# A hybrid decoder block: the output gate as four rounded-format matmuls, the three per-head sums as two each, and v centred while it is transposed

## The chip, the core and the metric

The kernel runs on one NeuronCore of one Trainium2 chip. The metric is the device time of one execution in microseconds (us); the time of before is the median of three runs.

## The reference, cut to what matters

One decoder block: an adaLN-modulated RMS norm, one input projection, two mixers side by side (RWKV-7 on 1024 channels, multi-window pooling on 1024), an output projection, a second norm, a gated MLP with a depthwise convolution, and a final norm. There are 512 tokens, a model width of 2048 and an MLP width of 5632, all in fp32. The change touches the RWKV-7 mixer (16 heads of 64 channels):

```python
kk = heads(k * k_k)
kk = kk / max(sqrt(sum(kk * kk, per head)), 1e-12)          # sum 1
...
y = _wkv7_scan(r, decay, k, v, -kk, kk * a)                 # per head a 64x64 state, linear in v
mean = mean(y, per head); var = mean((y - mean)**2, per head)   # sum 2
y = (y - mean) * rsqrt(var + 64e-5) * ln_w + ln_b
bonus = sum(r * k * r_k, per head) * v                      # sum 3
out = (y + bonus) * (sigmoid(xg) @ g2)                      # the gate; xg has 160 columns
```

## The kernel before

Channels lie on the 128 partitions, tokens along the free dimension, so a tile is 128x512. Two number formats go into TensorE. Plain fp32 operands are used as they are. Large projections use the rounded format fp32r: a weight tile is split into a rounded value `whi` (ScalarE cast, L106) and a remainder `wlo` (VectorE subtraction, L108), activations likewise, and one product is three matmuls of 512 columns (`mm3`, L111 to L114).

The program has three stages. First (L168 to L258) the modulation vectors are made on VectorE, x is normalised, and the first eight tiles of the input projection are summed in the eight PSUM banks `pf`. At its end (L235 to L258) ScalarE and VectorE empty those banks: the token-shifted `xwa`, `xg1`, `xg2` (the gate's 128 + 32 columns, through a sigmoid), the r, k, v tiles of the first pair, and two pooling inputs `upad`. The PSUM pool of the next stage takes over the same banks.

The second stage, from there to about 800 us, works through eight pairs of heads (p = 0 to 7). Per pair:
- `stage_a` (L358): loads the pair's LoRA weights `lw` (two buffers), makes the decay, then k's norm: square `sq` (ScalarE, L389), its sum over each head as a matmul with a block matrix of ones (`bones`, L391), Ln and Exp (L394, L395), then `ar`, `bt`, `nt`. A DRAM round trip and a serial chain of small VectorE operations (L421 to L430) invert a triangular part. The bonus is a second sum with `bones` (L449) times v.
- `stage_b` (L455): small matmuls that finish the inverse.
- `stage_c` (L511): four chunks of 128 tokens. Each transposes v, `bt`, `kt` (L520), multiplies by masks (L531) and carries the state. The result gathers in the PSUM tile `py` (tag "y"). Then the tail: copy `py` to SBUF (L577), subtract the head mean as a matmul with `cent` (L579), square (L581), sum with `bmean` (L583), Ln and Exp (L585, L586), scale (L587, L588), add the bonus (L589); the gate is two fp32 matmuls into the PSUM tile of tag "ch" (L591, L592), which the sum of L583 used just before; multiply (L593) and store to DRAM (L594).

Beside the pairs run the 27 remaining tiles of the input projection (`win_tile`, L314: 48 matmuls `mm` each) and the rest of the modulation vectors on VectorE (`ada_rest`, L334). The pairs' code stands under a high priority (L618); a scheduler fixes each engine's order before the run, and puts the `mm` matmuls where it finds room. Every engine works through its list strictly in that order, and so does SP, from which all DMAs are issued. Scratch tiles of the pairs come from one pool tag, `ring`, with seven buffers (L232).

The third stage, to the end at 2450 us, is the output projection, the MLP and the last norm; all of it is `mm3` work.

Of the kernel before, what the change touches and what calls it, by code (L numbers as in the profile page):

```python
# [9 lines left out]
F32 = mybir.dt.float32  # L10
F32R = mybir.dt.float32r
# [5 lines left out]
P = 128  # L17
T = 512
# [36 lines left out]
def block_kernel(ctx, tc, a, out, stop=None, dbg=None):  # L55
# [8 lines left out]
    nc.sync.dma_start(vec, a["vec"][:, :])  # L64
    cmat = cp.tile([P, 5, P], F32, tag="cmat", name="cmat")
    nc.sync.dma_start(cmat, a["cmat"][:, :, :])
    ident, bones, bmean, cent, ones = (cmat[:, i, :] for i in range(5))
    masks = cp.tile([P, 4, P], F32, tag="masks", name="masks")
    nc.sync.dma_start(masks, a["mask4"][:, :, :])
    mlev = cp.tile([P, 2, 64], F32, tag="mlev", name="mlev")  # L70
# [98 lines left out]
    if True:  # L169
# [53 lines left out]
        if True:  # L223
            def shift(ps, m, dst):
                S.activation(dst, ps, AF.Copy, scale=drv[:, m : m + 1])
                V.scalar_tensor_tensor(dst[:, 1:T], ps[:, 0 : T - 1], col("mu", m), dst[:, 1:T],
                                       op0=ALU.mult, op1=ALU.add)

            def ring(name):
                return ring16(name)[:, 16:]  # L230

            def ring16(name):  # L232
                return ra.tile([P, 16 + T], F32, tag="ring", name=name, bufs=7)
# [4 lines left out]
            xg1 = ra.tile([P, T], F32, tag="xg1", name="xg1")  # L238
            shift(pf[1], 25, xg1)
            S.activation(xg1, xg1, AF.Sigmoid)  # L240
            xg2 = ra.tile([P, T], F32, tag="xg2", name="xg2")
            shift(pf[2], 26, xg2)
            S.activation(xg2, xg2, AF.Sigmoid)

# [113 lines left out]
    def stage_a(p, rkv):  # L358
# [28 lines left out]

        sq = ring("sq")
        S.activation(sq, k, AF.Square, scale=col("kk", p))  # L389
        psn = atile()  # L390
        PE.matmul(psn, bones, sq, start=True, stop=True)  # L391
        inv = ring("inv")
        V.tensor_scalar_max(inv, psn, 1e-24)
# [17 lines left out]
        for h in range(2):  # L411
            V.tensor_mul(ntv[:, h, :, :], ch(pss[h]), masks[:, 0:1, :].to_broadcast([P, NC, P]))
        dn = tc.dram_tile([32, 32, 32], F32, name=f"dn{p}")
# [34 lines left out]
        psb = atile()  # L448
        PE.matmul(psb, bones, k2, start=True, stop=True)  # L449
        bv = q.bv = ra.tile([P, T], F32, tag="bv", name="bv", bufs=2)  # L450
# [60 lines left out]
    def stage_c(p, q):  # L511
        ar, bt, kt, v, y2 = q.ar, q.bt, q.kt, q.v, q.y2
        py = ctile("y")
        st = None
        for c in range(NC):
            cl = slice(c * P, (c + 1) * P)

            pst = btile()
            for i, src in enumerate((v, bt, kt)):
                PE.transpose(pst[:, i * P : (i + 1) * P], src[:, cl], ident)  # L520
# [9 lines left out]
            for h in range(2):  # L530
                V.tensor_mul(lc[:, h, :, :], pss[h][:, 0:384].rearrange("p (i t) -> p i t", i=3), masks[:, 1:4, :])  # L531

# [42 lines left out]

        y = ra.tile([P, T], F32, tag="post", name="y", bufs=2)
        S.copy(y, py)  # L577
        pyc = ctile("y")
        PE.matmul(pyc, cent, y, start=True, stop=True)  # L579
        sq = ra.tile([P, T], F32, tag="post", name="sqy", bufs=2)  # L580
        S.activation(sq, pyc, AF.Square)  # L581
        pv = ctile("ch")
        PE.matmul(pv, bmean, sq, start=True, stop=True)  # L583
        rs = ra.tile([P, T], F32, tag="post", name="rs", bufs=2)
        S.activation(rs, pv, AF.Ln, bias=eps[:, 1:2])  # L585
        S.activation(rs, rs, AF.Exp, scale=-0.5)  # L586
        V.tensor_mul(rs, pyc, rs)  # L587
# [3 lines left out]
        PE.matmul(pg, q.lw[:, 1, :], xg1, start=True, stop=False)  # L591
        PE.matmul(pg, q.lw[0:32, 2, :], xg2[0:32, :], start=False, stop=True)  # L592
        V.tensor_mul(rs, rs, pg)  # L593
# [294 lines left out]
def pack(x, c, w_ada, b_ada, norm1_g, w_in, mu_shift, w0, w2, a0, a2, g2, k_k, k_a, r_k, ln_x_w, ln_x_b,  # L888
# [16 lines left out]
    mu = np.zeros(27 * P, f)  # L905
    mu[: 3360] = A(mu_shift[0])
    put("mu", mu)
    put("w0", w0[0]); put("a0", a0[0]); put("kk", k_k[0]); put("ka", k_a[0]); put("rk", A(r_k[0]).reshape(-1))
# [17 lines left out]
    for i, n in enumerate(WIN_ORDER):  # L926
        w = 32 if n == "T2" else P
        blk[i, :, :, :w] = wi[:, starts[n] : starts[n] + w].reshape(KT, P, w)
    o["win0"] = C(blk[:8].transpose(1, 2, 0, 3)).reshape(KT, P, 8 * P)
# [15 lines left out]
    lora[:, :, 1, :] = A(g2[0])[:128].reshape(P, NP, P).transpose(1, 0, 2)  # L945
    lora[:, 0:32, 2, :] = A(g2[0])[128:].reshape(32, NP, P).transpose(1, 0, 2)
    o["lora"] = lora
# [4 lines left out]
    bo = (i[:, None] // 64 == i[None] // 64).astype(f)  # L952
    o["cmat"] = C(np.stack([eye, bo, bo / f(64), eye - bo / f(64), np.ones((P, P), f)], 1))
    lt = (i[:, None] < i[None]).astype(f)
    le = (i[:, None] <= i[None]).astype(f)
    o["mask4"] = C(np.stack([lt, le, lt, le], 1))
    ml = np.zeros((P, 2, 64), f)
# [26 lines left out]
```

## Time and profile before

| | us |
|---|---|
| median of 3 runs (2449.73 to 2455.32) | 2451.7 |
| profiled execution, its own time | 2452.14 |
| its span, first to last instruction | 2450.0 |
| TensorE (PE) busy in the span | 2347.1 |
| PE weight loads (PEld), which overlap | 1872.0 |
| VectorE (DVE) busy | 1408.7 |
| ScalarE (ACT) busy | 874.6 |

So 2.1 us of the profiled execution lie outside its span. A matmul's recorded length runs on into the next one, since matmuls are pipelined: the price of one is read from the distance between starts, not from its length. An fp32 matmul leaves two records, an fp32r matmul one, a transpose one. A number in square brackets behind a row of the timeline is the idle time ahead of it and who ended it.

### The profile page before, as it was taken

Reading aid. Unit: us, or ns where it says so; the run is one execution under the profiler, and the core shown is the slowest. Engines: PE = TensorE matmul, PEld = TensorE weight load, DVE = VectorE, ACT = ScalarE, POOL = GpSimd, SP = SyncE. Lnnn points to the kernel's source line nnn. Section 1 sums busy time; section 2 is a strip of 40 time slices with the busy share of each in tenths; the row PEclk is TensorE's granted clock in tenths of the full one; section 3 lists DMA queues with packets and bytes.
Section 4 is the critical chain, followed back from the end, with each engine's and each line's share of the span. In section 5 each row is a group of like instructions: output and inputs, shape, how many; then the busy total and the mean of one; then the engine's idle time right before and its main releaser. Section 6 shows DMA issues by size and latency. Waiting matters only on the chain.

```text
span 2450.0 us, 36089 instructions
## 1 busy us (share of the span) xinstructions
PE 2347.1 (96%) x13714; PEld 1872.0 (76%) x13714; DVE 1408.7 (57%) x2698; ACT 874.6 (36%) x1402; POOL 23.7 (1%) x29
## 2 busy tenths in 40 slices
PE   4889999999999999999999999999999999999997
PEld 3656666667667889887888888888888888888887
DVE  7987677787774357757534443444344434444457
ACT  3244443443433336532223322333233323323333
POOL 0000000000000002100000000000000000000000
PEclk9999999999999999999999999999999999999999
DMA  9975564556662635538533333333332333332335
GB/s 353 337 233 152 166 185 140 163 162 178 169 200 85 203 111 185 181 113 260 161 96 98 96 98 95 99 96 98 95 99 95 99 95 99 95 99 95 99 97 174
DMA packets 232160, 352.61 MB, mean 144 GB/s; under 512 B 74865, under 2 KB 80177, under 8 KB 227761
## 3 DMA queue, kind: packets, MB, share of 16 engines
q1 hardware_dynamic: 231986, 350.30, 46.0%
q8 instruction: 107, 1.75, 0.3%
q14 instruction: 67, 0.55, 0.1%
HBM read 334.22 MB, written 16.00 MB: 143 GB/s over the span
## 4 chain that ended last, share of the span: by engine, by line
PE 68%; DMA 3%; DVE 2%; ACT 1%; issue 0%; SPq 0%; POOL 0%; DVEq 0%; ACTq 0%; POOLq 0%
PE b L112 20%; PE b L114 20%; PE b L113 20%; DMA wraw<-wup 1%; PE mm L112 1%; PE mm L113 1%; PE mm L114 1%; DMA war<-ada 0%; PE pa L290 0%; DMA slot<-ada 0%; DMA wraw<-wdn 0%; DVE wlo L108 0%; DVE x L863 0%; PE pa L114 0%; PE pa L113 0%
## 5 line engine op out<-in xcount | busy, mean ns | idle before, releaser
L108 DVE TENSOR_TENSOR wlo<-wraw,whi 128x512 fp32r<-128x512 f32 x772 | 533.2, 692 | 694.9 <-ACT whi L106 679.6
L106 ACT CAST whi<-wraw 128x512 fp32r<-128x512 f32 x788 | 489.3, 622 | 1229.0 <-PE b L113 925.2
L114 PE MATMUL b<-hh,wlo 128*128 128x512 f32 (+1 forms) x1472 | 561.2, 381 | 5.9 <-DVE wlo L108 5.0
L112 PE MATMUL b<-hh,whi 128*128 128x512 f32 (+1 forms) x1472 | 560.0, 380 | 0.0
L113 PE MATMUL b<-hl,whi 128*128 128x512 f32 (+1 forms) x1472 | 559.5, 380 | 0.0
L112 PE MATMUL b<-ah,whi 128*128 128x512 f32 (+1 forms) x992 | 353.4, 357 | 4.3 <-ACT whi L106 2.5
L114 PE MATMUL b<-ah,wlo 128*128 128x512 f32 (+1 forms) x992 | 351.9, 355 | 0.8 <-DVE wlo L108 0.8
L113 PE MATMUL b<-al,whi 128*128 128x512 f32 (+1 forms) x992 | 352.1, 355 | 0.0
L114 PEld LDWEIGHTS b<-hh,wlo 128*128 128x128 f32 x1472 | 277.0, 188 | 62.1 <-DVE wlo L108 8.5
L112 PEld LDWEIGHTS b<-hh,whi 128*128 128x128 f32 x1472 | 276.9, 188 | 52.9 <-ACT whi L106 0.5
L113 PEld LDWEIGHTS b<-hl,whi 128*128 128x128 f32 x1472 | 277.0, 188 | 52.3
L112 PEld LDWEIGHTS b<-ah,whi 128*128 128x128 f32 x992 | 187.5, 189 | 33.7 <-ACT whi L106 4.3
L113 PEld LDWEIGHTS b<-al,whi 128*128 128x128 f32 x992 | 187.6, 189 | 27.4 <-DVE al L134 1.1
L114 PEld LDWEIGHTS b<-ah,wlo 128*128 128x128 f32 x992 | 187.6, 189 | 26.8 <-DVE wlo L108 1.2
L112 PE MATMUL mm<-ah,whi 128*128 128x512 f32 x464 | 192.4, 415 | 6.3 <-ACT upad L257 5.5
L113 PE MATMUL mm<-al,whi 128*128 128x512 f32 x464 | 191.8, 413 | 0.0
L114 PE MATMUL mm<-ah,wlo 128*128 128x512 f32 x464 | 190.1, 410 | 0.0
L343 DVE SCALAR_TENSOR_TENSOR jkr<-war,cq 128x512 bf16<-128x512 f32 x192 | 131.3, 684 | 18.7 <-DMA war<-ada 15.9
L848 DVE SCALAR_TENSOR_TENSOR x<-b,mod,x 128x512 f32<-128x512 f32 x80 | 59.7, 750 | 111.4 <-PE b L114 111.3
L112 PEld LDWEIGHTS mm<-ah,whi 128*128 128x128 f32 x464 | 88.4, 190 | 35.1 <-issue 10.4
L113 PEld LDWEIGHTS mm<-al,whi 128*128 128x128 f32 x464 | 88.3, 190 | 29.3 <-issue 13.0
L114 PEld LDWEIGHTS mm<-ah,wlo 128*128 128x128 f32 x464 | 88.4, 191 | 23.8 <-issue 6.3
(259 smaller groups left out, 2282.0 us busy)
## 6 DMA issues: line engine op xcount, KB each, us to landing
wraw<-wup SPq DMA_DIRECT2D x368, 256.0 KB, 3.0
war<-ada SPq DMA_DIRECT2D x192, 256.0 KB, 3.4
wraw<-wdn SPq DMA_DIRECT2D x192, 256.0 KB, 2.7
wraw<-win SPq DMA_DIRECT2D x140, 256.0 KB, 4.0
wa<-ada SPq DMA_DIRECT2D x32, 1024.0 KB, 6.9
wraw<-wout SPq DMA_DIRECT2D x88, 256.0 KB, 3.0
slot<-ada SPq DMA_DIRECT2D x64, 256.0 KB, 3.7
sp<-spill SPq DMA_DIRECT2D x21, 256.0 KB, 2.7
```

What stands on the lines that cost most here:

```text
L106: S.copy(hi, raw)
L108: eng.tensor_tensor(lo, raw, hi[:, :].bitcast(F32), op=ALU.subtract)
L112: PE.matmul(ps, wh, xh, start=start, stop=False)
L113: PE.matmul(ps, wh, xl, start=False, stop=False)
L114: return PE.matmul(ps, wl, xh, start=False, stop=stop)
L343: V.scalar_tensor_tensor(jk, wa, 1.0, cq[0], op0=ALU.mult, op1=ALU.mult, accum_out=modq[:, kq, j : j + 1])
L848: V.scalar_tensor_tensor(x2[f], ps, mod[:, 80 + f : 81 + f], x2[f], op0=ALU.mult, op1=ALU.add)
```

## The change

- A new helper `bsum(ps, x)` takes the place of the three sums' single fp32 matmul (L391, L449, L583). It rounds x to fp32r (`hi`, ScalarE), makes the remainder (`lo`, VectorE), and adds two fp32r matmuls with a block matrix of ones kept in fp32r (`bonesr`). `hi` and `lo` come from the `ring` tag.
- The gate's `xg1` and `xg2` are split once, at the end of the first stage; their projection and g2 weights now hold the 32-column part three times over, so that one 128-row matmul sums value times value, remainder times value and value times remainder. Per pair, `lw`'s gate part is copied into `gw` (ScalarE) and two remainders are taken (VectorE). The two fp32 matmuls become four fp32r ones.
- v is multiplied by `cent` in the matmul that transposed it, so `py` comes out centred: the copy of L577 and the matmul of L579 are gone, and the tail works on `py` itself. The factor 1/64 of `bmean` moves into the Ln.
- One mask and one constant matrix less are loaded (64 KB each), and the masks are addressed anew.

```diff
+    bonesr = cp.tile([P, P], F32R, tag="bonesr", name="bonesr")
+    S.copy(bonesr, bones)
...
+            def bsum(ps, x):
+                hi = ring16("hi", F32R)[:, 16:]
+                S.copy(hi, x)
+                lo = ring16("lo", F32R)[:, 16:]
+                V.tensor_tensor(lo, x, hi.bitcast(F32), op=ALU.subtract)
+                PE.matmul(ps, bonesr, hi, start=True, stop=False)
+                PE.matmul(ps, bonesr, lo, start=False, stop=True)
...
+            t, xg1h = gate_in(0)
+            xg1l = ra.tile([P, T], F32R, tag="xg1l", name="xg1l")
+            V.tensor_tensor(xg1l, t, xg1h[:, :].bitcast(F32), op=ALU.subtract)
+            t, xg2 = gate_in(1)
+            V.tensor_tensor(xg2[64:96, :], t[64:96, :], xg2[64:96, :].bitcast(F32), op=ALU.subtract)
...
-        PE.matmul(psn, bones, sq, start=True, stop=True)
+        bsum(psn, inv)
...
-        PE.matmul(psb, bones, k2, start=True, stop=True)
+        bsum(psb, k2)
...
+        gw = ra.tile([P, 3, P], F32R, tag="gw", name="gw")
+        S.copy(gw[:, 0:2, :], q.lw[:, 1:3, :])
+        V.tensor_tensor(gw[:, 2, :], q.lw[:, 1, :], gw[:, 0, :].bitcast(F32), op=ALU.subtract)
+        V.tensor_tensor(gw[32:64, 1, :], q.lw[32:64, 2, :], gw[32:64, 1, :].bitcast(F32), op=ALU.subtract)
...
-            for i, src in enumerate((v, bt, kt)):
+            PE.matmul(pst[:, 0:P], v[:, cl], cent, start=True, stop=True)
+            for i, src in ((1, bt), (2, kt)):
                 PE.transpose(pst[:, i * P : (i + 1) * P], src[:, cl], ident)
...
-        S.copy(y, py)
-        pyc = ctile("y")
-        PE.matmul(pyc, cent, y, start=True, stop=True)
-        sq = ra.tile([P, T], F32, tag="post", name="sqy", bufs=2)
-        S.activation(sq, pyc, AF.Square)
+        S.activation(rs, py, AF.Square)
         pv = ctile("ch")
-        PE.matmul(pv, bmean, sq, start=True, stop=True)
+        bsum(pv, rs)
...
-        PE.matmul(pg, q.lw[:, 1, :], xg1, start=True, stop=False)
-        PE.matmul(pg, q.lw[0:32, 2, :], xg2[0:32, :], start=False, stop=True)
+        PE.matmul(pg, gw[:, 0, :], xg1h, start=True, stop=False)
+        PE.matmul(pg, gw[:, 0, :], xg1l, start=False, stop=False)
+        PE.matmul(pg, gw[:, 2, :], xg1h, start=False, stop=False)
+        PE.matmul(pg, gw[:, 1, :], xg2, start=False, stop=True)
```

Since the scheduler lays the order out anew, three places of it are shown. The first is ScalarE at the end of the first stage; `pf` are the PSUM banks that it empties, `whi` the casts of weights for the `mm` matmuls of the second stage. Before:

```order
L237 ACTIVATE xwa<-xwa 64x512
L240 ACT_TABLE_LOAD
L240 ACTIVATE xg_1053<-xg_1053 128x512
L243 ACTIVATE xg_1057<-xg_1057 128x512
L225 ACTIVATE rkv<-pf_208,drv 128x512
L225 ACTIVATE rkv<-pf_209,drv 128x512
L225 ACTIVATE v<-pf_210,drv 128x512
L257 COPY upad<-pf_211 128x512
L257 COPY upad<-pf_212 128x512
L106 CAST whi<-wraw 128x512 x6
```

With the change (the line numbers are the new file's):

```order
L248 ACTIVATE xwa<-xwa 64x512
L532 CAST gw<-lw 128x256
L252 ACT_TABLE_LOAD
L252 ACTIVATE xg<-xg 128x512 x2
L254 CAST xgh_1059<-xg 128x512
L254 CAST xgh_1067<-xg 128x512
L227 ACTIVATE rkv<-pf_210,drv 128x512
L227 ACTIVATE rkv<-pf_211,drv 128x512
L227 ACTIVATE v<-pf_212,drv 128x512
L276 COPY upad<-pf_213 128x512
L108 CAST whi<-wraw 128x512 x2
L276 COPY upad<-pf_214 128x512
```

Ahead of the copy that empties the last bank there are now the cast of the first pair's gate weights, the two casts of the gate's inputs, and two weight casts that stood behind it.

The second is TensorE at the tail of the pair p = 2. Before, from the matmul with `cent` on, with `y` for the result, `sqy` for its square and `xg` for the gate:

```order
L579 MATMUL y<-y,cmat 128x512
L114 MATMUL mm<-ah_536,wlo 128x512
L112 MATMUL mm<-ah_588,whi 128x512
L113 MATMUL mm<-al_589,whi 128x512
L114 MATMUL mm<-ah_588,wlo 128x512
L583 MATMUL ch<-sqy,cmat 128x512
L112 MATMUL mm<-ah_640,whi 128x512
L113 MATMUL mm<-al_641,whi 128x512
L114 MATMUL mm<-ah_640,wlo 128x512
L112 MATMUL mm<-ah_692,whi 128x512
L591 MATMUL ch<-xg_1053,lw 128x512
L592 MATMUL ch<-xg_1057,lw 128x512
```

With the change, from the matmul that sums the rounded squares on:

```order
L243 MATMUL ch<-hi,bonesr 128x512
L114 MATMUL mm<-ah_746,whi 128x512
L115 MATMUL mm<-al_747,whi 128x512
L116 MATMUL mm<-ah_746,wlo 128x512
L244 MATMUL ch<-lo,bonesr 128x512
L114 MATMUL mm<-ah_798,whi 128x512
L115 MATMUL mm<-al_799,whi 128x512
L116 MATMUL mm<-ah_798,wlo 128x512
L114 MATMUL mm<-ah_850,whi 128x512
L609 MATMUL ch<-xgh_1059,gw 128x512
L610 MATMUL ch<-xg1l,gw 128x512
L611 MATMUL ch<-xgh_1059,gw 128x512
```

The matmul with `cent` is gone, two matmuls with `bonesr` stand where one with `bmean` stood, with three `mm` matmuls between value and remainder. The gate comes four `mm` matmuls behind the sum in both; it is now four matmuls, of which the last stands behind the rows shown.

The third is SP's list of DMAs where the LoRA weights of the pair p = 2 are loaded. Before, behind the loads of that pair's v and next to the store of the first pair's result:

```order
L104 DMA wraw<-win 128x512
L341 DMA war<-ada 128x512
L612 DMA v<-sp_2_1881 128x512
L341 DMA war<-ada 128x512 x11
L362 DMA lw<-lora 128x384
L341 DMA war<-ada 128x512
L594 DMA mixd_95<-rs 128x512
```

With the change, far ahead of that place, between the stores of the first pooling group and the load of the next pair's r:

```order
L314 DMA mixd_111<-mxp 128x512
L360 DMA war<-ada 128x512 x2
L314 DMA mixd_112<-mxp 128x512
L381 DMA lw<-lora 128x384
L360 DMA war<-ada 128x512 x4
L106 DMA wraw<-win 128x512 x2
L360 DMA war<-ada 128x512
L632 DMA rkv<-sp_0_1509 128x512
```

The gate reads `gw`, not `lw`, so a buffer of `lw` comes free once it is copied, and no longer at the end of the pair; the loads of the later pairs move one pair ahead in the same way.

More of the change, by code (lines that the diff above doesn't have):

```diff
@@ L906, in pack @@
     mu[: 3360] = A(mu_shift[0])
+    mu[3360:3424] = np.tile(mu[3328:3360], 2)
     put("mu", mu)
@@ L945, in pack @@
     lora[:, :, 1, :] = A(g2[0])[:128].reshape(P, NP, P).transpose(1, 0, 2)
-    lora[:, 0:32, 2, :] = A(g2[0])[128:].reshape(32, NP, P).transpose(1, 0, 2)
+    for c in range(3):
+        lora[:, 32 * c : 32 * c + 32, 2, :] = A(g2[0])[128:].reshape(32, NP, P).transpose(1, 0, 2)
     o["lora"] = lora
```

48 lines of the change are left out of this document (24 added, 24 removed).

## The prediction

> **What bounds the kernel now.** I read the page's slices first, then busy time by stage, then the waits, then matmul starts on the timeline. The span and three rows of the slices (40 equal slices, busy tenths):
>
> ```profile
> span 2450.0 us, 36089 instructions
> ...
> PE   4889999999999999999999999999999999999997
> ...
> DVE  7987677787774357757534443444344434444457
> ...
> PEclk9999999999999999999999999999999999999999
> ```
>
> TensorE is nearly always busy from the fourth slice on. The change sits in slices 3 to 13, where VectorE is busy too, so that stretch needs its own numbers. Two stages of the busy-time table, one pair's period and the end of the last pair, and their sum over nine stages from 185 to 805 us (columns: us, busy us of PE, PEld, DVE, ACT, POOL, clock, DMA share, GB/s):
>
> ```profile
> 467.00:531.00 64.00, 64.00 (x640) 42.54 (x640) 48.81 (x117) 29.03 (x44) 0.00 (x0) 1.00 0.56 163
> ...
> 752.00:805.00 53.00, 52.11 (x204) 38.26 (x204) 22.49 (x41) 23.35 (x36) 0.00 (x0) 0.97 0.37 115
> sum 620.00, PE 600.05 PEld 414.88 DVE 444.16 ACT 256.24 POOL 0.00; mean PE 66.67 PEld 46.10 DVE 49.35 ACT 28.47 POOL 0.00
> ```
>
> PE is busy 600 of 620 us, DVE 444 (72%), ACT 256 (41%). Who waits for whom says the same: the longest wait of the stage (244 to 735 us; total, times, longest) is ACT's for a weight buffer that PE still reads.
>
> ```profile
> ACT whi L106 <- PE mm L113: 74.3, 42, 5.4
> ```
>
> The last question is whether the pairs' chain or PE's total work ends the stage. The six pooling tiles of the projection are evacuated at L646, and the eight pairs' results are finished at L593; the rows give first and last start:
>
> ```profile
> L646 ACT COPY upad<-mm x6: 578/580/587, 693.2 to 790.9; 128x512 f32<-128x512 f32 x6
> L593 DVE TENSOR_TENSOR rs<-rs,ch x8: 671/686/687, 293.0 to 762.3; 128x512 f32<-128x512 f32 x8
> ```
>
> The last pair is done at 762 us, and `mm` work lasts until 791. So PE's work, not the chain, ends the stage, and what PE saves shortens it, as long as PE doesn't wait more than now.
>
> **Prices on PE.** The tail of the pair p = 1:
>
> ```profile
> 328.16 0.39 PE L112 MATMUL mm<-ah,whi 128*128 128x512 f32 x1
> 328.39 1.02 PE L579 MATMUL y<-y,cmat 128*128 128x512 f32 x2
> 328.85 0.80 PE L113 MATMUL mm<-al,whi 128*128 128x512 f32 x1
> 329.49 0.39 PE L114 MATMUL mm<-ah,wlo 128*128 128x512 f32 x1
> ...
> 330.19 1.04 PE L583 MATMUL ch<-sqy,cmat 128*128 128x512 f32 x2
> 330.66 0.80 PE L114 MATMUL mm<-ah,wlo 128*128 128x512 f32 x1
> 331.30 0.40 PE L112 MATMUL mm<-ah,whi 128*128 128x512 f32 x1
> ...
> 333.06 1.13 PE L591 MATMUL ch<-xg,lw 128*128 128x512 f32 x2 [0.90 <-ACT rs L585]
> 334.12 1.12 PE L592 MATMUL ch<-xg,lw 32*128 32x512 f32 x2
> 335.17 0.50 PE L112 MATMUL mm<-ah,whi 128*128 128x512 f32 x1
> 335.50 0.40 PE L113 MATMUL mm<-al,whi 128*128 128x512 f32 x1
> ```
>
> An fp32r matmul takes 0.23 us (328.16 to 328.39). The fp32 one of L579 and one `mm` take 1.10 (328.39 to 329.49), so it takes 0.87; L583 likewise 1.11 - 0.23 = 0.88. The two gate matmuls, with nothing to overlap, take 2.11 (333.06 to 335.17). The first fp32r one after such a gap takes 0.33, 0.10 more than the next. The two sums with `bones` have no such clean neighbours; their records:
>
> ```profile
> L449 PE MATMUL pa<-k,cmat 128*128 128x512 f32 x16 | 9.6, 687 | 0.5 <-DVE nt L412 0.5
> L391 PE MATMUL pa<-sq,cmat 128*128 128x512 f32 x16 | 8.4, 607 | 0.1
> ```
>
> They lie between 0.87 and 1.05 (half of 2.11); I take the middle, 0.96 each. **Removed per pair:** 0.87 + 0.88 + 2.11 + 2 x 0.96 = 5.78 us.
>
> Added: six fp32r matmuls for the sums and four for the gate, 10 x 0.23, and one entry of 0.10. v with `cent` is an fp32 matmul of 128 columns, two records where the transpose had one:
>
> ```profile
> 309.69 0.33 PE L520 MATMUL pb<-cmat,v 128*128 128x128 f32 x1
> 309.86 0.27 PE L520 MATMUL pb<-cmat,bt 128*128 128x128 f32 x1
> 309.97 0.27 PE L520 MATMUL pb<-cmat,kt 128*128 128x128 f32 x1
> ```
>
> Records of this size follow each other by 0.11 (0.17 for the first), so four chunks cost 0.44 more. **Added per pair:** 2.30 + 0.10 + 0.44 = 2.84. The difference, 2.94 us, times eight is **-23.5 us**; with 0.87 or 1.05 for the sums it is -22.1 or -24.9.
>
> **What ACT and DVE get.** A remainder and a cast of this size, and two ScalarE copies of 384 and 128 columns:
>
> ```profile
> L108 DVE TENSOR_TENSOR wlo<-wraw,whi 128x512 fp32r<-128x512 f32 x95 | 65.0, 686 | 42.2 <-ACT whi L106 32.1 <-PE mm L114 7.3 <-DMA war<-ada 2.0
> L106 ACT CAST whi<-wraw 128x512 fp32r<-128x512 f32 x95 | 58.7, 618 | 140.2 <-PE mm L113 97.6 <-DMA wraw<-win 21.4 <-DVE wlo L108 7.2
> L522 ACT COPY tok<-pb 128x384 f32<-128x384 f32 x32 | 15.3, 479 | 48.4 <-PE pb L520 48.2
> L542 ACT COPY R<-ch 128x128 f32<-128x128 f32 x32 | 8.5, 266 | 52.1 <-PE ch L539 52.1
> ```
>
> Per pair ACT gets three casts of 0.62 and the 256-column cast of `gw`, 0.37 (midway between 0.27 and 0.48), and loses the copy of L577; that is under 2.3 us, or 18 in all. DVE gets three remainders of 0.69 and two small ones, at most as long as that and more likely near a third of it: 2.1 to 3.5 us, about 20 in all. As busy time this is hidden under PE: DVE goes from 72% to (444 + 20) of about 602, or 77%. The masks' multiply keeps its size, and 128 KB less to load at the start I cost at nothing. As latency it is not free: PE meets the matmul of `lo` in its list, and all behind it stands still until the remainder is there. The nearest row is the sum of before, L583, which waited for one ACT step behind four `mm` matmuls. Its weight load's idle time, over eight pairs:
>
> ```profile
> L583 PEld LDWEIGHTS ch<-sqy,cmat 128*128 128x128 f32 x16 | 2.4, 188 | 1.7 <-ACT sqy L581 1.7
> ```
>
> 1.7 us in eight is 0.2 each. For `lo` the order shows three `mm` matmuls of cover (0.7 us) against a remainder of 0.69. At 0.2 for each of 24 sums, PE waits **+4.8 us** more. The upper end is a whole remainder each, 24 x 0.69 = 16.6. The lower one is below nothing: the tail's chain is laid out anew, and if the 0.90 us ahead of L591 (333.06, above) went in every pair, that would be -7.2.
>
> **The handover of the banks.** PE stands still until the last bank is empty (PE's start in the second stage, ACT's last copy and next casts, the clock while PE restarts):
>
> ```profile
> 155.56 0.39 PE L114 MATMUL pf<-ah,wlo 128*128 128x512 f32 x1
> 161.44 0.76 PE L112 MATMUL mm<-ah,whi 128*128 128x512 f32 x1 [5.48 <-ACT upad L257]
> 162.00 0.63 PE L113 MATMUL mm<-al,whi 128*128 128x512 f32 x1
> ...
> 166.26 0.50 PE L114 MATMUL mm<-ah,wlo 128*128 128x512 f32 x1
> ...
> 161.18 1.17 ACT L106 CAST whi<-wraw 128x512 fp32r<-128x512 f32 x2
> ...
> 162.00:167.00 5.00, 5.00 (x14) 3.94 (x13) 5.00 (x11) 0.85 (x2) 0.00 (x0) 0.55 0.48 154
> ```
>
> ACT's list now has ahead of that last copy two casts for the gate, two weight casts (1.1 us each two, since they overlap a little) and one `gw` cast of 0.37: **+2.6 us** on the path, with nothing to cover it. From 162.00 to 166.26 PE ran at half rate, 10 matmuls at 0.43 where 0.23 is usual, some 2 us. A second stretch of that kind is the worst end, 0 the best (if the weight casts that come earlier are repaid behind): 0 to 4.6.
>
> [...]
>
> **The LoRA weights.** PE's first matmuls of a pair wait for `lw`; the idle time of all who read it (total, times), and L367's own:
>
> ```profile
>   DMA lw<-lora: 5.2, 5
> ...
> L367 PE MATMUL pa<-xwa,lw 64*128 64x512 f32 x14 | 8.0, 653 | 2.0 <-DMA lw<-lora 2.0
> ```
>
> The load moves a pair ahead, so this goes: **-2.0 us**; 0 if another wait is late next (ACT's Ln, ahead of the gate, isn't touched), 5.2 at most. The loads of r and k move the other way, since 11 `ring` tiles per pair now share seven buffers; I cost that at nothing, because the place of `nt` in PE's list hardly moves.
>
> **Sum:** -23.5 + 4.8 + 2.6 - 2.0 = -18.1 us against the profiled execution's 2452.1 (2450.0 and 2.1 outside): 2434.0. The median, 2451.7, is 0.4 lower, which I leave aside.
>
> **Rivals.**
> 1. The sums' chain becomes the bound, and the kernel is slower. Mechanism: at each sum PE waits for a cast and a remainder, 0.62 + 0.69 = 1.31 us, because DVE's list holds other work ahead of `lo`: 24 x 1.31 = 31.4, so -23.5 + 31.4 + 2.6 - 2.0 = +8.5, or **2460.6 us**. It decides from (23.5 - 2.6 + 2.0) / 24 = 0.95 us of wait per sum. For it: DVE is 72% busy, and PE has such waits.
>
> ```profile
> PE pa L409 <- DVE bt L401: 4.1, 2, 2.2
> ```
>
> That is two waits, the longest of 2.2 us. Against it: the sums of before hardly waited (0.1 and 0.5 us of idle time in the rows of L391 and L449), and `mm` matmuls stand in between. Chance 0.11.
> 2. The gain is eaten: the pairs' latency holds the `mm` work back, PE idles where it had matmuls to do, and the stage ends as before, **2452 us**. For it: the casts lengthen each pair's chain. Against it: 29 us of `mm` work lie behind the last pair (762 to 791), more than the gain. Chance 0.11.
> 3. The rounded matmuls cost as much as fp32: ten at 0.87 instead of 0.23 add 6.4 us per pair, 51 in all, **2485 us**. The `mm` rows at 0.23 are in this format; chance under 0.01.
>
> **How the numbers follow.** The forecast, 2434.0, has 0.78. Its own range: low -24.9 - 5.2 - 7.2 + 0 = -37.3, or 2415; high -22.1 + 16.6 + 4.6 + 0 = -0.9, or 2451. The second rival lies at its upper edge, so 2415 to 2452 leaves out the first rival and little else. About 0.2% (4.9 us) is what a measurement of this kernel tells from no change. Faster by more than that: 0.78; within it: 0.11; slower: 0.11.
>
> **What would show it.** In the profile after: the gate's four matmuls about 0.23 us apart; no copy of `py`; PE's first `mm` at about 164 us instead of 161.4, with the half-rate stretch behind it; no wait of L367 for `lw`; the waits for `lo` under 0.5 us each; the last pair's result and the last pooling evacuation each some 18 us earlier. The prediction is wrong if PE's waits for `lo` or for casts sum to over 20 us, if DVE's busy share in the pairs' stage passes 85%, or if the evacuations of L646 don't move although the gate got shorter.

## The result and the profile after

| | before | after |
|---|---|---|
| median, us (4 runs each) | 2451.1 | 2518.1 |
| lowest to highest | 2449.7 to 2455.3 | 2512.7 to 2524.5 |
| ratio, 95% interval | | 1.0278 [1.0262, 1.0294] |
| profiled execution, its span | 2452.1, 2450.0 | 2524.5, 2522.7 |
| mean granted TensorE clock | 0.992 | 0.959 |
| TensorE at half rate, in all | 43.3 us | 210.6 us |
| PE idle between 185 and 900 us | 20.9 us | 37.3 us |

The kernel became 67 us slower, where 18 us faster was forecast. The half-rate time is the sum of the stretches in which the trace's record of the granted clock stands at 0.5 (it knows only 0.5 and 1), up to the end of the execution, some 2 us behind the last instruction. The page's slices of after (span, busy tenths of PE and DVE, clock in tenths):

```profile
span 2522.7 us, 36191 instructions
...
PE   4779999999998999999999999999999999999997
...
DVE  7988777666575435865744443444334444444447
...
PEclk9989999788786999999999999999999999999999
```

PE looks as full as before. What has changed is the last row: 6 to 8 tenths in the slices 8 to 13, where before has 9s throughout. Between 400 and 900 us the stretches in which PE ran at half rate begin at 440.3, 515.4, 529.0, 607.5, 706.5 and 761.1 us and last 34.1, 3.4, 20.5, 51.2, 17.1 and 47.8 us. Busy time by stretch, in the columns of the prediction; first `stage_c` of the pair p = 3 of before, from the end of its `stage_b` to its gate:

```profile
446.50:473.00 26.50, 26.50 (x221) 16.16 (x218) 21.18 (x75) 9.15 (x18) 0.00 (x0) 1.00 0.58 165
```

The same stretch of after, the whole pairs' stage, and its last half-rate stretch:

```profile
442.90:487.70 44.80, 44.79 (x256) 29.18 (x256) 27.53 (x82) 13.70 (x23) 0.00 (x0) 0.65 0.37 102
185.00:865.00 680.00, 642.65 (x5469) 462.19 (x5468) 455.31 (x1178) 265.63 (x412) 0.00 (x0) 0.87 0.50 144
...
761.10:808.90 47.80, 42.26 (x430) 31.95 (x432) 24.93 (x67) 4.74 (x12) 0.00 (x0) 0.50 0.40 126
```

With no idle time in either, the same stage takes 44.8 us where it took 26.5: the clock is 0.65 where it was 1.00 (0.87 over the whole pairs' stage). The two aren't quite the same work (256 records on PE, not 221): 31.5 us of the stretch are at half rate, so the clock's part of the 18.3 us is about half of that, 15.7. The gate came as forecast. That of the last pair and its neighbours on PE:

```profile
813.53 0.50 PE L609 MATMUL ch<-xgh,gw 128*128 128x512 f32 x1 [0.82 <-ACT rs L603]
813.87 0.39 PE L610 MATMUL ch<-xg1l,gw 128*128 128x512 f32 x1
814.10 0.40 PE L611 MATMUL ch<-xgh,gw 128*128 128x512 f32 x1
814.33 0.40 PE L612 MATMUL ch<-xgh,gw 128*128 128x512 f32 x1
814.57 0.39 PE L116 MATMUL mm<-ah,wlo 128*128 128x512 f32 x1
```

That is 1.04 us instead of 2.11. But the pooling evacuations (first and last start behind the durations), 693.2 to 790.9 before, start together with the end of the last pair:

```profile
L666 ACT COPY upad<-mm x6: 578/581/590, 810.4 to 865.1; 128x512 f32<-128x512 f32 x6
```

Now some waits of the pairs' stage, 185 to 870 us (total, times, longest), in after:

```profile
PE pb L526 <- ACT Tm L523: 6.6, 4, 2.6
PE pb L480 <- DMA x<-dxz: 5.5, 6, 2.5
PE pa L427 <- DVE bt L419: 3.6, 3, 1.7
PE pb L521 <- DVE x L513: 3.3, 5, 1.0
...
PE pa L244 <- DVE lo L242: 0.8, 1, 0.8
```

PE hardly waits for `lo`, which the prediction watched. It waits at the end of stage_b: L521 makes the tile that ScalarE copies to `Tm` (L523), and L526 uses it. The same wait in before:

```profile
PE pb L508 <- ACT Tm L505: 0.2, 1, 0.2
```

The longest of these waits in after, in time order, ScalarE and PE:

```profile
605.31 1.28 ACT L412 ACT_TABLE_LOAD   x1
606.56 1.19 PE L521 MATMUL pb<-x,nt 64*64 64x64 f32 x16 [1.03 <-DVE x L513]
606.61 0.63 ACT L412 ACTIVATE inv<-inv 128x512 f32<-128x512 f32 x1
607.14 0.60 ACT L240 CAST hi<-k 128x512 fp32r<-128x512 f32 x1
607.76 1.28 ACT L413 ACT_TABLE_LOAD   x1
609.06 0.63 ACT L413 ACTIVATE inv<-inv 128x512 f32<-128x512 f32 x1
609.71 0.58 ACT L523 COPY Tm<-pb 64x512 f32<-64x512 f32 x1
610.34 1.97 PE L526 MATMUL pb<-y,Tm 64*64 64x64 f32 x16 [2.59 <-ACT Tm L523]
```

The next pair's Ln and Exp with their table loads, and the new cast, stand ahead of `Tm`; no `mm` matmul stands between L521 and L526. PE idles 1.03 and 2.59 us, and the 16 matmuls of L526 take 1.97 us where those of L521 took 1.19: the clock fell at 607.5, with the first of the two waits behind it and the second just ahead (L521 ends at 607.75), and came back at 658.7. Of the five stretches of 17 us and more, three begin at these two waits (440.3, 529.0, 607.5). The one at 706.5 begins behind a wait for `bt` (L427, 1.27 us), and the last pair's, at 761.1, soon behind one of 2.50 us for the DMA load that L480 reads.

### The profile page after: what moved, and what is told of

Its sections match the earlier page's. It is cut to its first block, busy times and chain, and to the rows that moved or that the text cites. A ratio compares the mean times of both kernels' runs of the same rounds, so it can differ in the third digit from the quotient of the medians.

```text
span 2522.7 us, 36191 instructions
## 1 busy us (share of the span) xinstructions
PE 2399.8 (95%) x13730; PEld 1926.4 (76%) x13730; DVE 1426.2 (57%) x2740; ACT 889.3 (35%) x1431; POOL 24.4 (1%) x29
## 3 DMA queue, kind: packets, MB, share of 16 engines
q1 hardware_dynamic: 231986, 350.17, 44.8%
## 4 chain that ended last, share of the span: by engine, by line
PE 83%; DVE 7%; DMA 4%; ACT 3%; issue 2%; SPq 0%; POOL 0%; DVEq 0%; ACTq 0%; POOLq 0%
PE b L114 19%; PE b L116 19%; PE b L115 19%; PE mm L116 3%; PE mm L114 3%; PE mm L115 3%; DVE jk L206 2%; PE pb L552 2%; PE pb L550 1%; DVE wlo L110 1%; PE pb L541 1%; PE y L592 1%; PE pa L427 1%; PE pa L309 1%; PE ch L562 1%
```

## The experiments

H is the half-rate time of a profiled execution. At half rate about half of the time is lost (an `mm` matmul took 0.43 us, not 0.23, at the handover), so the span less H/2 is about what it would have been at full clock. "None between" are the pairs (of 0 to 7) in whose order no `mm` matmul stands between the group that makes `Tm` and the group that uses it (L521 and L526 after, L503 and L508 before). Times are medians in us, each ratio against runs of before taken along with it.

| kernel | time | ratio, 95% interval | H | span - H/2 | none between |
|---|---|---|---|---|---|
| before | 2451.1 | | 43.3 | 2428.4 | no pair |
| after | 2518.1 | 1.0278 [1.0262, 1.0294] | 210.6 | 2417.4 | 3 4 5 6 7 |
| w1_warm | 2508.8 | 1.0235 [1.0208, 1.0263] | 147.8 | 2435.2 | dummies there |
| p_sums | 2486.9 | 1.0157 [1.0139, 1.0175] | 115.0 | 2425.9 | 4 5 6 7 |
| p_gate | 2442.0 | 0.9976 [0.9964, 0.9987] | 40.1 | 2419.9 | no pair |
| p_cent | 2452.0 | 1.0017 [1.0006, 1.0027] | 38.1 | 2428.7 | no pair |
| r_tailown | 2484.2 | 1.0165 [1.0138, 1.0192] | 128.5 | 2418.4 | 3 4 5 6 |
| r_bring | 2473.8 | 1.0114 [1.0092, 1.0137] | 82.7 | 2432.6 | 7 |
| s_two | 2463.0 | 1.0063 [1.0045, 1.0080] | 83.8 | 2422.5 | 0 4 |
| s_tail | 2470.5 | 1.0103 [1.0084, 1.0123] | 78.8 | 2428.8 | 7 |
| f_fill10 | 2473.4 | 1.0102 [1.0087, 1.0117] | 72.9 | 2439.0 | filled |
| n_norm32 | 2455.6 | 1.0028 [1.0006, 1.0050] | 42.6 | 2428.3 | 5 |
| n_gatecent | 2446.9 | 0.9992 [0.9982, 1.0001] | 42.6 | 2423.7 | no pair |
| b_tm3 | 2465.8 | 1.0069 [1.0046, 1.0091] | 67.1 | 2431.9 | 6 |
| n_bonus32 | 2485.0 | 1.0159 [1.0129, 1.0189] | 128.5 | 2423.0 | 3 4 5 6 |
| n_gct | 2457.3 | 1.0033 [1.0021, 1.0046] | 49.1 | 2430.8 | no pair |
| n_gct_tvec | 2451.0 | 1.0012 [1.0003, 1.0021] | 51.9 | 2422.6 | no pair |

The spans reach over 83 us (2439.9 to 2522.7), the spans less H/2 over 22. So most of the differences between the spans is half-rate time. By that column the kernel after has 11 us *less* to do than before.

### First theories: the clock, and which part

Theory C was that the halved clock is the loss, theory W that the waits of the longer chains are, and the clock only a companion. Dummy matmuls in the gaps of stage_b were to tell them apart, and the three parts were run alone.

w1_warm:

```diff
+    def warm(ps):
+        for _ in range(3):
+            PE.matmul(ps, bonesr, H[0][0], start=True, stop=True)
...
+        warm(pT)
...
+        warm(pT)
...
+        warm(pY)
```

> The kernel after, with 9 more fp32r matmuls of 512 columns per pair and nothing else: three ahead of each of the three groups of small matmuls of stage_b that start a PSUM tile behind a wait. Their results are overwritten, so only TensorE work is added: 72 x 0.23 = 16.6 us. Theory C (clock): the profiled loss of the kernel after is the halved TensorE clock (210 us at half rate against 43 before, so some 85 us lost), which waits of 1 to 2.6 us among the small matmuls set off; with the gaps filled the half-rate time falls below 100 us and the time to 2440 to 2465, although work is added. Theory W (waits): the time goes into the longer chain of the sums, and the clock only follows; then the added work can only cost: 2518 to 2535.

2508.8 us, H 147.8: as time it is neither. The dummies write into the tile of the group behind them, and so waited for that tile's buffer themselves (total, times, longest):

```profile
PE pb L475 <- DVE x L518: 9.5, 6, 2.9
```

The last pair still had no `mm` matmul beside its stage_b. H fell by 63 us and the work grew by 16.6, which the span less H/2 accounts for (2417.4 to 2435.2), but as a test it is inconclusive.

p_sums takes over only `bsum` and its three uses (and the 1/64 in the Ln):

```diff
-        PE.matmul(psn, bones, sq, start=True, stop=True)
+        bsum(psn, sq)
...
-        PE.matmul(psb, bones, k2, start=True, stop=True)
+        bsum(psb, k2)
...
-        PE.matmul(pv, bmean, sq, start=True, stop=True)
+        bsum(pv, sq)
```

> The kernel before with the three sums as two rounded matmuls each (and the 1/64 in the Ln), with the gate and the centring of before. If the sums bring the loss (their casts and remainders stand ahead of stage_b's copies on ScalarE and VectorE, and the order of the mm matmuls changes with them): 2490 to 2530, with 150 us or more at half rate. If the gate's part or the interplay of all three brings it: sums removed 2 x 0.96 + 0.88 = 2.80 per pair, added 6 x 0.23 = 1.38, so -11.4 us, +4.8 us of waits: 2445 (2438 to 2455).

p_gate takes over only the gate with its operands (and the tail's scratch in one buffer, not two, to make room for them):

```diff
-        PE.matmul(pg, q.lw[:, 1, :], xg1, start=True, stop=False)
-        PE.matmul(pg, q.lw[0:32, 2, :], xg2[0:32, :], start=False, stop=True)
+        PE.matmul(pg, gw[:, 0, :], xg1h, start=True, stop=False)
+        PE.matmul(pg, gw[:, 0, :], xg1l, start=False, stop=False)
+        PE.matmul(pg, gw[:, 2, :], xg1h, start=False, stop=False)
+        PE.matmul(pg, gw[:, 1, :], xg2, start=False, stop=True)
```

> The kernel before with the gate in four rounded matmuls, with the sums and the centring of before. If the sums bring the loss: the gate's 2.11 us become 4 x 0.23 + 0.10 = 1.02, so -8.7 us, +2.6 at the handover of the banks, -2.0 for the earlier load of the LoRA weights: 2443 (2438 to 2450), half-rate time as before (43 us, under 70). If the earlier load of the LoRA weights brings it (the next pair's stage_a runs into stage_b of the pair before): 2490 to 2530 here and not in the kernel with the sums alone.

p_cent takes over only the centring:

```diff
-            for i, src in enumerate((v, bt, kt)):
+            PE.matmul(pst[:, 0:P], v[:, cl], cent, start=True, stop=True)
+            for i, src in ((1, bt), (2, kt)):
...
-        S.copy(y, py)
-        pyc = ctile("y")
-        PE.matmul(pyc, cent, y, start=True, stop=True)
+        pyc = py
```

> The kernel before with v times the centring matrix in place of v's transpose, and without the copy of the result and the matmul with the centring matrix; sums and gate as before. On TensorE -0.87 + 0.44 = -0.43 us per pair, so -3.4 us, and one ScalarE copy less in the tail's chain: 2447 (2440 to 2452) if this part is innocent; over 2460 if the changed tail lets TensorE fall to half rate by itself.

The sums bring the loss: 2486.9, 38.6 us over its before (2448.3), with H 115; both are somewhat less than the 2490 and the 150 expected. The gate saves 6.4 us (8.7 by its matmuls). The centring is 3.7 us slower where 3.4 faster was expected, at H 38. The three add to 36 us and the change lost 67. In the change five pairs have none between, not four as in p_sums; whether that is the other 31 us, no run shows.

### Where the sums lose: the ring, or the latency

`hi` and `lo` come from the tag `ring`, and so do `upad` and the next pairs' r and k. Theory R: the tail's two ring tiles, which stand ahead of `upad` in the program, keep it from a buffer; so the two `mm` banks stay full and the last pair runs without cover. Theory L: the casts and remainders make the waits by their time.

r_tailown, on after:

```diff
-            def bsum(ps, x):
+            def bsum(ps, x, own=False):
...
-                hi = ring16("hi", F32R)[:, 16:]
+                hi = ra.tile([P, T], F32R, tag="kt", name="hi", bufs=2) if own else ring16("hi", F32R)[:, 16:]
...
-                lo = ring16("lo", F32R)[:, 16:]
+                lo = ra.tile([P, T], F32R, tag="bt", name="lo", bufs=2) if own else ring16("lo", F32R)[:, 16:]
...
-        bsum(pv, rs)
+        bsum(pv, rs, True)
```

> The kernel after with one change: the value and the remainder of the tail's sum (the sum of the squared result) come from the buffers of kt and bt, which that pair has done with, and no longer from the pool tag ring. Every instruction is the same. Theory R (ring): buffers of a tag are given out in the order of the program, so in the kernel after the loads of the next pairs' r and k, and the copies that empty the pooling tiles, can't have a ring buffer before the tail of the pair ahead has had its two; both mm banks stay full, no mm matmul stands beside the last pair, and TensorE waits and falls to half rate. Then the order has 1173 of the 1392 mm matmuls ahead of the last pair's gate again (after 1109, before 1179), the half-rate time falls under 80 us (after 211, before 43) and the time to 2430 to 2455. Theory L (latency): the casts and remainders themselves, on the path of the pairs and in ScalarE's list ahead of stage_b's copies, make the waits; they are all still there, so 2495 to 2525.

r_bring, on before:

```diff
-        y = ra.tile([P, T], F32, tag="post", name="y", bufs=2)
+        y = ring("y")
...
-        sq = ra.tile([P, T], F32, tag="post", name="sqy", bufs=2)
+        sq = ring("sqy")
```

> The kernel before with one change: the tail's copy of the result and its square (y and sqy) come from the pool tag ring and not from a tag of their own. No instruction is added or taken away, no rounded sum is in it. Theory R: it loses as the kernel after does, 2480 to 2525 with over 90 us at half rate, since the order has 1108 mm matmuls ahead of the last pair's gate where before has 1179. Theory L: 2446 to 2455, as before, since nothing is longer.

s_two and s_tail split the edit of p_sums. s_two:

```diff
-        PE.matmul(psn, bones, sq, start=True, stop=True)
+        bsum(psn, sq)
...
-        PE.matmul(psb, bones, k2, start=True, stop=True)
+        bsum(psb, k2)
```

> The kernel before with the two sums of stage_a (k's norm and the bonus) as two rounded matmuls each, the tail's sum in fp32, gate and centring as before. Theory R: the tail asks the ring tag for nothing, so no loss: 8 x 2 x (0.96 - 0.46) = 8.0 us less on TensorE, at most 16 x 0.2 = 3.2 of waits back: 2443 (2436 to 2452). Theory L: two of the three casts and remainders are here, and they are the ones ahead of stage_b's copies: 2470 to 2490.

s_tail:

```diff
-        PE.matmul(pv, bmean, sq, start=True, stop=True)
+        bsum(pv, sq)
```

> The kernel before with the tail's sum alone as two rounded matmuls, whose value and remainder come from the pool tag ring. Theory R: this is the whole loss of the kernel with all three sums (which took 38.5 us more than before) and a little more, as the saving of stage_a's sums is missing: 2480 to 2510. Theory L: one of three sums, in the tail and not ahead of stage_b: 2445 to 2460.

r_bring adds no instruction and loses 26.8 us (2473.8 against 2446.95). On ScalarE, its last pair's tail and the first two evacuations of `upad`:

```profile
753.10 0.59 ACT L577 COPY y<-y 128x512 f32<-128x512 f32 x1 [1.44 <-PE y L571]
754.90 0.60 ACT L581 ACTIVATE sqy<-y 128x512 f32<-128x512 f32 x1 [1.21 <-PE y L579]
755.39 1.07 ACT L646 COPY upad<-mm 128x512 f32<-128x512 f32 x2
```

The two copies stand right behind the tail's two ring tiles, as in after (810.4, above); before had the first at 693.2. From 707.2 us on, 41 us of half rate follow. The other way round, r_tailown has them early again:

```profile
L666 ACT COPY upad<-mm x6: 566/580/589, 728.6 to 824.5; 128x512 f32<-128x512 f32 x6
...
741.40:790.00 48.60, 46.40 (x565) 31.46 (x564) 32.61 (x84) 13.32 (x25) 0.00 (x0) 1.00 0.54 175
```

Its last pair (the second row, a stretch) runs at full clock, and it is 30 us nearer to before than after is (37.2 over, not 67.0). So the ring is shown, and it is nearly half of the loss, not the whole that theory R expected. All four kernels came out between the ranges of the two theories, each of which put the whole loss down to one cause. s_tail, the tail's sum alone, loses 23.5 us, with one long stretch, in the last pair (30.7 us from 708.6); with the 16.1 of s_two that makes 39.6, and p_sums lost 38.6. That a buffer is given out in program order is how I read the order, not a thing that was measured.

What is left in r_tailown are four stretches of 17 to 37 us, which begin at 437.8, 516.3, 594.9 and 687.0, in the pairs 3 to 6, the first three at the waits of L521 and L526, the last at one of 2.70 us for `bt` (L427); s_two, whose tail asks nothing of the ring, loses 16 us and has two stretches. Of theory L remains that the sums of stage_a do something of their own. Its last two groups of the pair 5 in r_tailown:

```profile
589.62 0.63 ACT L412 ACTIVATE inv<-inv 128x512 f32<-128x512 f32 x1
591.12 1.14 PE L521 MATMUL pb<-x,nt 64*64 64x64 f32 x16 [1.03 <-DVE x L513]
592.50 0.63 ACT L413 ACTIVATE inv<-inv 128x512 f32<-128x512 f32 x1
593.15 0.58 ACT L523 COPY Tm<-pb 64x512 f32<-64x512 f32 x1
593.78 1.14 PE L526 MATMUL pb<-y,Tm 64*64 64x64 f32 x16 [1.52 <-ACT Tm L523]
```

### Is it the clock, and is it the norm

f_fill10 fills these two waits of r_tailown with dummies that wait for nobody:

```diff
+        fill = ctile("y")
+        with tc.issue_after(lastX.ins):
+            for _ in range(4):
+                PE.matmul(fill, bonesr, H[0][0], start=True, stop=True)
...
+        fill = ctile("y")
+        with tc.issue_after(lastT.ins):
+            for _ in range(6):
+                PE.matmul(fill, bonesr, H[0][0], start=True, stop=True)
```

> The kernel r_tailown with ten more fp32r matmuls of 512 columns per pair at the end of stage_b, into a PSUM bank that is free there and that nobody reads: four right behind the group ahead of L521 (where TensorE waits for VectorE's x), six right behind the group of L521 (where TensorE waits for ScalarE's copy Tm). They fill these two waits and change nothing else: 80 x 0.23 = 18.4 us more work on TensorE, of which the waits hide at most 10. Theory C (clock): the half-rate stretches of r_tailown (17, 17, 37 and 17 us, each beginning at one of these waits) don't begin; half-rate time from 128 us to under 65, some 40 us of loss gone: 2484 + 18 - 10 - 40 = 2452 (2440 to 2468). Theory W (waits): halved clock or not, the waits themselves are what is lost, so more work can only be hidden in them: 2484 to 2500.

n_norm32 puts one sum of r_tailown back:

```diff
-        bsum(psn, inv)
+        PE.matmul(psn, bones, inv, start=True, stop=True)
```

> The kernel r_tailown with the sum of k's norm as one fp32 matmul again (bonus and tail sum rounded, gate and centring as in the kernel after). Theory N (norm): the cast, the remainder and the second matmul stand in the serial chain from k's square to Ln, Exp and bt, and push Ln and Exp on ScalarE in front of stage_b's copy Tm, and the mm matmuls out from between L521 and L526. The order has none there in the pairs 3 to 6 of r_tailown, and 4, 8, 7, 8, 7, 0, 2, 4 here: one half-rate stretch at the pair 5 at most, half-rate time 40 to 80 us, 2435 to 2456. Rival B (bonus): the cast of the bonus's k, which stands near that copy on ScalarE, is the one in the way; it is still here: 2475 to 2490.

n_gatecent is n_norm32 with the other two sums put back as well:

```diff
-        bsum(psb, k2)
+        PE.matmul(psb, bones, k2, start=True, stop=True)
...
-        bsum(pv, rs, True)
+        PE.matmul(pv, bones, rs, start=True, stop=True)
```

> The kernel after with all three sums as one fp32 matmul each: only the gate in parts and the centred v are left. In the order at least one mm matmul stands between L521 and L526 in every pair (5, 8, 4, 8, 7, 8, 1, 4), so half-rate time as before, 35 to 60 us, and the sum of the two parts measured alone, -6.4 and +3.7: 2444 (2436 to 2450). If the gate's earlier load of the LoRA weights or the shorter tail were part of the loss: over 2460.

b_tm3 delays the copy in before:

```diff
         S.copy(Tm[64:128], r8(pT)[64:128])
+        S.copy(Tm[64:128], r8(pT)[64:128])
+        S.copy(Tm[64:128], r8(pT)[64:128])
+        S.copy(Tm[64:128], r8(pT)[64:128])
```

> The kernel before with ScalarE's copy Tm (64x512, L505) made four times in a row into the same tile; nothing rounded, no other tag. TensorE needs the last copy, so it comes about 1.5 us later. The order puts 5, 26, 15, 10, 10, 17, 0, 12 mm matmuls between the two groups on its two sides (before: 4, 6, 4, 1, 13, 1, 4, 4). Theory C: only in the pair with 0 does TensorE stand still, some 2 us, and there a half-rate stretch of 15 to 50 us begins: 2447 + 2 + 8 to 25 = 2457 to 2474, half-rate time 55 to 95 us. Theory W: 8 x 1.5 = 12 us at most, less what the mm matmuls hide, and no stretch at half rate: 2447 to 2455.

f_fill10 does 18.4 us more work and is 10.8 us faster than r_tailown (2473.4 and 2484.2, or 24 and 37 over their before), which theory W excludes. Its groups of the pair 3 and of the pair 5:

```profile
443.19 1.65 PE L531 MATMUL y<-ah,bonesr 128*128 128x512 f32 x6
444.77 0.56 PE L534 MATMUL pb<-y,Tm 64*64 64x64 f32 x6
...
589.72 1.66 PE L531 MATMUL y<-ah,bonesr 128*128 128x512 f32 x6
591.30 0.33 PE L534 MATMUL pb<-y,Tm 64*64 64x64 f32 x2
...
594.88 0.48 PE L558 MATMUL pb<-ar,bt 64*128 64x128 f32 x2 [0.67 <-ACT y L535]
```

No wait is left at `Tm`, and three of the four stretches are gone, that of the pair 6 too, where the six dummies now stand ahead of L427. It still missed theory C's 2440 to 2468: one stretch (30.7 us from 595.4 on) began all the same, a few us later, behind a wait of 0.67 us, and hardly any of the 18.4 us was hidden (2418.4 to 2439.0 in the last column but one).

n_norm32 has no long stretch left in its profiled execution, which took 2451.3 us at a mean clock of 0.992. Of its ten runs the two around the median had 0.986, which is an estimated 30 us more at half rate (2 x 0.006 x 2450). The pair 5 on ScalarE and PE there:

```profile
575.53 0.63 ACT L413 ACTIVATE inv<-inv 128x512 f32<-128x512 f32 x1
576.07 0.60 ACT L108 CAST whi<-wraw 128x512 fp32r<-128x512 f32 x1
576.58 0.61 ACT L240 CAST hi<-k 128x512 fp32r<-128x512 f32 x1
...
578.84 0.58 ACT L523 COPY Tm<-pb 64x512 f32<-64x512 f32 x1 [0.85 <-PE pb L521]
579.61 0.76 PE L526 MATMUL pb<-y,Tm 64*64 64x64 f32 x10 [0.81 <-DVE y L515]
```

Exp (L413) starts 3.3 us ahead of the copy; in r_tailown it starts 0.65 us ahead and holds it up. The cast of the bonus's k is in both (in r_tailown at 590.57). n_norm32 also shows the clock by itself: ten runs of the one program took 2442.1 to 2467.7 us, the fastest at a mean clock of 0.993, the slowest at 0.983. That is 25.6 us, and 0.010 of some 2450 us is 24.5.

n_gatecent came out at 2446.9, within its range; it also keeps the tail's `rs` in one buffer, where before had two, so that part of the change costs nothing either. b_tm3 lost 16.6 us as theory C expected (2457 to 2474), but not where it expected it: its pair 6 waited 1.41 us at `Tm` without a fall, and its pair 0, with five `mm` matmuls between, waited 2.00 us there, and at the end of that wait 17 us at half rate began (267.0). So a wait added without any rounding can set off half rate; which wait does it isn't read from the order alone.

### What was still open

n_bonus32 is the counterpart of n_norm32 (the bonus back to fp32, the norm rounded):

```diff
-        bsum(psb, k2)
+        PE.matmul(psb, bones, k2, start=True, stop=True)
```

> The kernel r_tailown with the sum of the bonus as one fp32 matmul again (k's norm and the tail's sum rounded): the counterpart of n_norm32. Theory N (norm): the sum of k's norm is what pushes Ln and Exp in front of the copy Tm; it is still here, and the order has 2, 8, 5, 0, 0, 0, 0, 5 mm matmuls between L521 and L526: half-rate stretches in some of the pairs 3 to 6, 90 to 140 us in all, 2470 to 2490. Theory B (bonus): the rounded sum of the bonus counts as much: 2445 to 2462. By the span less half of the half-rate time (2418 for r_tailown, 2428 for n_norm32) it should come to 2418 to 2428 either way.

n_gct puts both sums of stage_a of r_tailown back:

```diff
-        bsum(psn, inv)
+        PE.matmul(psn, bones, inv, start=True, stop=True)
...
-        bsum(psb, k2)
+        PE.matmul(psb, bones, k2, start=True, stop=True)
```

> The kernel after with the two sums of stage_a in fp32 again and the tail's sum rounded, its value and remainder in the buffers of kt and bt. The order has mm matmuls between L521 and L526 in every pair (5, 9, 7, 8, 1, 7, 7, 5) and 1184 of them ahead of the last pair's gate: half-rate time 35 to 60 us. n_gatecent with one of the three sums rounded, 8 x (0.88 - 0.46) = 3.4 us less on TensorE, less some waits for the remainder: 2445 (2438 to 2450). If the longer tail alone, with fillers in place, still lets TensorE fall to half rate: over 2455.

n_gct_tvec also moves the copy:

```diff
-        S.copy(Tm[64:128], r8(pT)[64:128])
+        V.tensor_copy(Tm[64:128], r8(pT)[64:128])
```

> The kernel n_gct with the copy Tm (L523) on VectorE in place of ScalarE. Nothing of Ln and Exp can stand ahead of it there, and the order has 8, 6, 17, 8, 16, 10, 10, 8 mm matmuls between L521 and L526. If TensorE's remaining waits at that copy cost anything: 2 to 8 us less than n_gct, 2440 (2434 to 2446). If the place is harmless once matmuls cover it: the same as n_gct.

n_bonus32 took 2485.0, as slow as r_tailown, with the same H of 128.5: it is the norm's sum, not the number of sums. The slices of its clock:

```profile
PEclk9999999889989999999999999999999999999998
```

n_gct took 2457.3, above its 2438 to 2450, where its second case was put (over 2455), but at the H of the first, 49. Its waits have other causes:

```profile
PE pa L309 <- DMA pw<-poolw: 5.8, 1, 5.8
PE pa L410 <- ACT inv L408: 4.2, 4, 1.6
PE mm L116 <- DVE wlo L110: 3.4, 3, 1.7
```

A load of the pooling weights came 5.8 us late at the end of the stage (767.1); the reason stays open. With the copy on VectorE it is 6.3 us faster, as the expectation's first case had it, yet at 2451.0 not the 2440. No version found beats the gate alone (p_gate, 2442.0, 0.9976 of before).

## Why the prediction was wrong

Two things failed: the ring, which was put at nothing, and the price of a wait, which was taken as its length. By the prediction's own steps:

- **Work on PE, -23.5 us: the mechanism was right.** The gate takes 1.04 us (forecast 1.02), the sums' matmuls follow at 0.23. The span less H/2 fell by 11.0 although PE's idle time between 150 and 900 us grew by 19.5 (26.6 to 46.1), so the work itself shrank by an estimated 24 (the idle time inside the half-rate stretches, 14.2 us against 1.8, is halved in that column though it costs in full: 11.0 - 6.2 + 19.5 = 24.3). Measured alone, the gate gave 6.4 of its 8.7 us and the centring was 3.7 us slower; the sums' share shows in this estimate only.
- **Waits for `lo`, +4.8: right as far as it went.** They came to 0.8 us. The mistake is the place: the remainder's time was charged to PE's wait at the matmul of `lo`, but k's norm goes on from there to Ln, Exp and `bt`. Later, Ln and Exp land ahead of stage_b's `Tm` in ScalarE's list (Exp ends at 609.69, `Tm` starts at 609.71), and PE waits for that, 6.6 us in four times, where before had `mm` matmuls to do and waited 0.2. n_norm32 and n_bonus32 show it: some 31 us of the loss (37.2 over before to 6.3) hang on this one sum. That the place of Ln and Exp ahead of `Tm` is the link is read from the timelines (0.65 us ahead, or 3.3); no run moved only that copy while the norm's sum was rounded.
- **The ring, costed at nothing: the step that failed.** The prediction saw that eleven ring tiles would share seven buffers, and set the price to nothing because `nt` hardly moved on PE's list. It looked at the loads of r and k and not at `upad`, which stands behind the last pair's tail in the same tag. r_bring shows the price with nothing else changed: 26.8 us; taking it out of after gave 30 back.
- **Handover of the banks, +2.6: right.** The first `mm` starts at 164.48 (forecast 164), 3.0 us later than before, and the half rate around it lasts 10.2 us instead of 6.8, of which PE works 6.1 and 5.0. There the text had half rate before its eyes, and took it for a matter of that place. It counted each wait in the stage at its length. In fact 1.0 to 2.1 us of waits among the small matmuls, in the 3.41 us ahead of each of the five stretches, were followed by 17 to 51 us at half rate. This is the size that failed: H/2 grew by 84 us, and with the 11 us gained it gives 73 of span.
- **The LoRA weights, -2.0: right.** No PE wait for `lw` is left.
- **The rivals.** The first named a slower kernel through waits of the sums' chain and gave 2460.6. Its direction was right and its place wrong: PE waits for the sums' casts 3.7 us in all (L243, 2.4 and 1.3), and with `lo` 4.5, not 31.4. The second had PE idle where it had matmuls to do; that happened beside the last pair, but the price was more than the gain that it was put at. The third fell: the rounded matmuls take 0.23 us. The signs that were to prove the prediction wrong: the L666 evacuations moved 74 us the wrong way; DVE was at 67% (455.3 of 680 us), far from 85%.

Two things stay open: why the three parts together lose 31 us more than the sum of the parts (the table shows more pairs without cover, no more), and what decides how long a stretch lasts.

## What to carry over

In this kernel the long matmuls between the small ones were cover for the clock as much as for the time: in after, 1.0 to 2.1 us of waits among small matmuls were followed by 17 to 51 us at half rate, and ten dummies per pair in f_fill10 took three of the four such stretches of r_tailown away. So before costing a wait by its length, see what stands between it and the nearest long matmuls. A new scratch tile from a shared tag is a dependence on everything that takes this tag behind it in the program, and its price is found where the last of those stands. A step on a serial chain is priced at the far end of the chain, in the list of the engine that goes on from there.

## What the hardware showed that was not expected

In the 17 profiles all half-rate stretches of the pairs' stage last multiples of 3.41 us (3.4, 6.8, 10.2, 17.1, 20.5, ...), and in one profile their starts lie whole multiples apart (in after 354.9 - 160.4 = 57 x 3.413). Cutting 190 to 800 us of these profiles into windows of 3.41 us on that grid and adding PE's idle time in each gives, for the windows at full rate:

| idle in the window, us | windows | followed by half rate |
|---|---|---|
| under 1.3 | 2715 | 7 |
| 1.3 to 1.6 | 40 | 12 |
| over 1.6 | 50 | 46 |

So in these profiles about half a window of idleness was enough nearly every time (46 of 50 above 1.6 us). In before, a wait of 1.87 us inside one window (193.88 to 195.75) was followed by 3.4 us at half rate from 197.2 on, and one of 2.20 us that lay across an edge (217.04 to 219.24, the edge at 217.67) by none; no run shows that the edge made the difference. The longest single wait of PE in after's pairs' stage is 2.59 us; H/2 grew by 84 us all the same. The idle time is not all of it. Between 1.3 and 1.6 us, 10 of 14 windows with fewer than three `mm` matmuls were followed by half rate, and 2 of 26 with more. All seven cases under 1.3 us had fewer than three, and two of them had no idle time on record at all (in n_bonus32 ahead of 13.7 us from 299.0 on, in f_fill10 ahead of 6.8 from 301.9 on). Back at full rate came 34 of 37 half-rate windows with three or more `mm` matmuls in them, and 30 of 211 with fewer, though 200 of those 211 have under 1.3 us of idle time. So what moves the clock isn't PE's busy time as recorded; what it is stays open.
